# Rotary embedding on one core: table loads moved to SyncE's queue, four small transfers added on ScalarE's

## The chip, the core and the metric

The kernel runs on one core of a Trainium2 chip. The metric is the device time of one execution in microseconds (us), lower is better. The span of a profile, from its first to its last instruction, is a little shorter than that time. Five engines take part: TensorE (PE in the profile), VectorE (DVE), ScalarE (ACT), GpSimd (POOL) and SyncE (SP). Sixteen DMA engines move data between HBM and the on-chip memory. A transfer is issued by one of the instruction engines into its own queue: SyncE's is q1 in the profile, ScalarE's is q10.

## What is computed

```python
# x: (16, 512, 1024) float32, cos and sin: (512, 32) float32, 16 heads of 64
x = x.reshape(batch, seq, num_heads, head_dim)
x1, x2 = x[..., :half_dim], x[..., half_dim:]
cos, sin = cos[None, :, None, :], sin[None, :, None, :]
rotated = np.concatenate([x1 * cos - x2 * sin, x1 * sin + x2 * cos], axis=-1)
```

Every head's vector of 64 is split into two halves of 32, which are rotated by an angle that depends on the position alone. 33.5 MB are read and 33.5 MB are written; the two tables have 64 KB each.

## The kernel before

x is cut into eight tiles of 4 MB. A tile has 128 partitions (2 batches of 64 row groups), and each partition holds 8 rows (k) of 1024 numbers. Five tile buffers exist, so the first five tiles are loaded at once, and the last three wait for the stores of the first three tiles. The result is written over the tile and stored from there.

```python
NB = 2
BUFS = 5
PE_ROWS = ((0, 4), (0, 4))   # rows whose sum is made by TensorE
DVE_B = ((0,), (0,))         # row whose sin product is made by VectorE
FIRST = (3, 8)               # the first tile is loaded in two parts: 3 rows, then 5
LAST_OUT = (4, 8)            # the last tile is stored in two halves
# [...] views, pools
    load(0, 0, FIRST[0])                                      # L73: nc.sync.dma_start
    sin_sb = bp.tile([P, dim], FP32, name="b")[:PB, : KK * half]
    cos_sb = bp.tile([P, dim], FP32, name="b")[:PB, : KK * half]
    nc.scalar.dma_start(out=sin_sb, in_=sin_v)                # L82
    nc.scalar.dma_start(out=cos_sb, in_=cos_v)                # L83
    for lo, hi in zip(FIRST, FIRST[1:]):
        load(0, lo, hi)
    for t in range(1, BUFS):
        load(t)
```

The tables are spread over the 128 partitions by TensorE, with a matrix that repeats each of 64 rows twice; VectorE then makes a signed copy of the sin table. Everything after that needs these tables.

```python
    nc.tensor.matmul(out=sin_t, lhsT=spread, rhs=sin_sb, start=True, stop=True)    # L104
    nc.tensor.matmul(out=cos_t, lhsT=spread, rhs=cos_sb, start=True, stop=True)    # L105
    nc.vector.tensor_scalar_mul(out=sns[:, :, 0, :], in0=sin_k, scalar1=-1.0)      # L107
    nc.vector.tensor_copy(out=sns[:, :, 1, :], in_=sin_k)                          # L108
```

In the main loop GpSimd multiplies a row, with its halves swapped, by the signed sin table (L165). VectorE multiplies by cos (L183) and adds the two (L145). For rows 0 and 4 of each tile the sum is made by TensorE in PSUM (L178) and copied back by ScalarE (L179); for row 0 VectorE makes the sin product as well (L176).

```python
    for t in range(NT):                     # NT = 8 tiles
        xt = tiles[t]
        for k in range(KK):                 # KK = 8 rows
            # [...] the row's work, as above
            if k == 0 and t > 0:
                finish(t - 1)               # store of tile t-1; after tile 2's, the loads of tiles 5 to 7
            add(1)
    finish(NT - 1)

    def store(t, lo=0, hi=KK):
        s = slice(lo * dim, hi * dim)
        nc.sync.dma_start(out=out_v[t][:, s], in_=tiles[t][:, s])                  # L77
```

All loads of x and all stores are issued by SyncE, in program order.

Of the kernel before, what the change touches and what calls it, by code (L numbers as in the profile page):

```python
# [8 lines left out]
FP32 = mybir.dt.float32  # L9
# [12 lines left out]

FIRST = (3, 8)
LAST_OUT = (4, 8)


@with_exitstack
def kernel(
# [13 lines left out]
    nc = tc.nc  # L42
# [7 lines left out]
    NT = batch // NB  # L50
# [4 lines left out]
    cos_v = cos.rearrange("(p k) j -> p (k j)", k=KK)  # L55
    sin_v = sin.rearrange("(p k) j -> p (k j)", k=KK)

    fixed = ctx.enter_context(tc.tile_pool(name="fixed", bufs=1))
# [10 lines left out]
    def load(t, lo=0, hi=KK):  # L69
        if tiles[t] is None:  # L70
            tiles[t] = xp.tile([P, F], FP32, name="xt")
        s = slice(lo * dim, hi * dim)
        nc.sync.dma_start(out=tiles[t][:, s], in_=x_v[t][:, s])  # L73
# [5 lines that stand above are left out]
    load(0, 0, FIRST[0])  # L79
    sin_sb = bp.tile([P, dim], FP32, name="b")[:PB, : KK * half]  # L80
    cos_sb = bp.tile([P, dim], FP32, name="b")[:PB, : KK * half]
    nc.scalar.dma_start(out=sin_sb, in_=sin_v)  # L82
    nc.scalar.dma_start(out=cos_sb, in_=cos_v)  # L83
    for lo, hi in zip(FIRST, FIRST[1:]):
        load(0, lo, hi)
    for t in range(1, BUFS):
# [6 lines left out]
    for i in range(3):  # L93
        ps = pe.tile([P, BANK], FP32, name="ps")
        nc.tensor.matmul(out=ps, lhsT=zero[:, :P], rhs=zero, start=True, stop=True)  # L95

    sns = fixed.tile([P, KK, 2, half], FP32)
    tab = pfix.tile([P, BANK], FP32)
    cos_t = tab[:, : KK * half]
# [14 lines left out]
    def cos_b(k, n):  # L114
        c = cos_t[:, k * half : (k + 1) * half]
        return bass.AP(tensor=c.tensor, offset=c.offset, ap=[c.ap[0], [0, n], [1, half]])

    def over_heads(s):
        return bass.AP(tensor=s.tensor, offset=s.offset, ap=[s.ap[0], [0, nh], [1, hd]])

    def swapped(r, n):
        return bass.AP(
            tensor=r.tensor, offset=r.offset + half, ap=[r.ap[0], [hd, n], [-half, 2], [1, half]]
        )

    def swapped_signed(k):

        i = on_dve.index(k)
        s = sns_t[:, i * hd : (i + 1) * hd]
        return bass.AP(  # L130
            tensor=s.tensor, offset=s.offset + half, ap=[s.ap[0], [0, nh], [-half, 2], [1, half]]
        )

    def pairs(r):
        return r.rearrange("p (a j) -> p a j", j=half)

    def halves(r):
        return r.rearrange("p (h a j) -> p h a j", a=2, j=half)
# [3 lines left out]
    def add(most):  # L142
        while len(pending) > most:
            r, ps, b = pending.pop(0)
            nc.vector.tensor_tensor(out=r, in0=ps, in1=b, op=ALU.add)  # L145

    def finish(t):
        add(0)
        lo = 0
        for hi in LAST_OUT if t == NT - 1 else (KK,):  # L150
            store(t, lo, hi)
            lo = hi
        if t + 1 == NT - BUFS:
            for n in range(BUFS, NT):
                load(n)

    for t in range(NT):
        xt = tiles[t]
        for k in range(KK):
            r = xt[:, k * dim : (k + 1) * dim]  # L160
            own = k in DVE_B[t % 2]
            if not own:
                b = bp.tile([P, dim], FP32, name="b")
                sk = sns[:, k].rearrange("p a j -> p (a j)")
                nc.gpsimd.tensor_tensor(out=halves(b), in0=swapped(r, nh), in1=over_heads(sk), op=ALU.mult)  # L165
            if k in PE_ROWS[t % 2]:
                parts = []
                for c in range(0, dim, BANK):
                    ps = pe.tile([P, BANK], FP32, name="ps")
                    rc = r[:, c : c + BANK]  # L170
                    nc.vector.tensor_tensor(  # L171
                        out=pairs(ps), in0=pairs(rc), in1=cos_b(k, BANK // half), op=ALU.mult
                    )
                    parts.append((ps, rc, swapped(rc, BANK // hd) if own else b[:, c : c + BANK]))
                if own:
                    nc.vector.tensor_tensor(out=halves(r), in0=halves(r), in1=swapped_signed(k), op=ALU.mult)  # L176
                for ps, rc, rhs in parts:
                    nc.tensor.matmul(out=ps, lhsT=ident, rhs=rhs, start=False, stop=True, skip_group_check=True)  # L178
                    nc.scalar.copy(out=rc, in_=ps)  # L179
            else:  # L180
                add(1)
                ps = pd.tile([P, dim], FP32, name="pd")
                nc.vector.tensor_tensor(out=pairs(ps), in0=pairs(r), in1=cos_b(k, 2 * nh), op=ALU.mult)  # L183
                pending.append((r, ps, b))
            if k == 0 and t > 0:
                finish(t - 1)
            add(1)
    finish(NT - 1)


# [33 lines left out]
```

## Time and profile before

| what | value | from |
|---|---|---|
| time, median of 3 | 165.22 us (165.15 to 165.28) | the times |
| span of the profiled execution | 163.5 us | page, first line |
| VectorE busy | 141.4 us (86%) | page, part 1 |
| GpSimd busy | 130.3 us (80%) | page, part 1 |
| TensorE busy | 62.6 us (38%) | page, part 1 |
| ScalarE busy | 20.0 us (12%) | page, part 1 |
| moved | 67.26 MB, mean 411 GB/s | page, part 2 |
| sin table, issue to landing | 7.3 us | page, part 6 |
| cos table, issue to landing | 10.9 us | page, part 6 |
| last two stores of 2 MB, issue to landing | 7.2 us (median) | page, part 6 |

Busy times of different engines lie beside each other and don't add up. A group of instructions is shown with its line in the kernel, its engine, what it writes and reads, its count, its busy time, and in brackets the idle time of the engine ahead of it with what ended that idle time. "DMA" in such a bracket is the landing of a transfer. The chain that ended last is followed back from the last instruction; here it holds VectorE's lines 183, 145, 171 and 176, and the wait at the close of the program (L219). For a window of the span, the profile gives each engine's busy time, the granted TensorE clock, the mean busy share of the 16 DMA engines and what they moved; a packet counts in the window in which it starts.

### The profile page before, as it was taken

The numbers are of one execution on the slowest core, as the hardware profiler recorded it, in microseconds if no ns is written. First come the engines' busy times: TensorE is split into PE (matmuls) and PEld (weight loads), VectorE is DVE, ScalarE is ACT, GpSimd is POOL, SyncE is SP. The second block draws the span as 40 slices with busy tenths as digits, with TensorE's granted clock in tenths as the row PEclk, the third lists the DMA queues.
The fourth block names the chain that finished last, engine by engine and source line by source line (L and its number), as shares of the span: only waits on it lengthen the run. The fifth ranks groups of instructions, "written<-read, shape, count | busy, mean of one in ns | idle before, by whom it ended". The sixth has DMA issues, their size and how long they took to land. (4 is left out here: it accounts for less than half of the span.)

```text
span 163.5 us, 523 instructions
## 1 busy us (share of the span) xinstructions
PE 62.6 (38%) x71; PEld 19.9 (12%) x71; DVE 141.4 (86%) x142; ACT 20.0 (12%) x33; POOL 130.3 (80%) x62
## 2 busy tenths in 40 slices
PE   3022736071804453172608090546217350809000
PEld 0011211020202020111102020202011200202000
DVE  1006999999999999999999999999999999999900
ACT  0210112011110202020201110021102020112000
POOL 1004999999999999999999999998999979970000
PEclk9999999659555555555555559576856786585555
DMA  5999999999989999999999999999999999999994
GB/s 186 443 393 420 489 409 393 497 393 425 473 385 457 441 387 481 409 401 497 361 393 401 489 393 459 425 385 393 393 465 425 425 457 401 393 401 393 433 397 196
DMA packets 2754, 67.26 MB, mean 411 GB/s; under 512 B 320, under 2 KB 448, under 8 KB 448
## 3 DMA queue, kind: packets, MB, share of 16 engines
q1 hardware_dynamic: 2592, 67.11, 97.0%
q10 hardware_dynamic: 160, 0.13, 0.2%
q14 instruction: 2, 0.02, 0.0%
HBM read 33.69 MB, written 33.55 MB: 411 GB/s over the span
## 5 line engine op out<-in xcount | busy, mean ns | idle before, releaser
L165 POOL TENSOR_TENSOR b<-xt,sns 128x1024 f32<-128x1024 f32 x56 | 129.6, 2355 | 15.5 <-DVE sns L108 13.1
L183 DVE TENSOR_TENSOR pd<-xt,tab 128x1024 f32<-128x1024 f32 x48 | 58.1, 1225 | 0.8
L145 DVE TENSOR_TENSOR xt<-pd,b 128x1024 f32<-128x1024 f32 x48 | 58.3, 1217 | 0.0
L178 PE MATMUL ps<-xt,ident 128*128 128x512 f32 x32 | 29.5, 1078 | 48.9 <-issue 45.0
L178 PE MATMUL ps<-b,ident 128*128 128x512 f32 x32 | 29.2, 1067 | 29.7 <-DVE ps L171 27.2
L179 ACT COPY xt<-ps 128x512 f32<-128x512 f32 x32 | 18.7, 586 | 124.1 <-PE ps L178 124.1
L171 DVE TENSOR_TENSOR ps<-xt,tab 128x512 f32<-128x512 f32 x32 | 20.5, 687 | 0.0
L178 PEld LDWEIGHTS ps<-xt,ident 128*128 128x128 f32 x32 | 9.4, 324 | 68.0 <-issue 63.4
L178 PEld LDWEIGHTS ps<-b,ident 128*128 128x128 f32 x32 | 9.2, 317 | 49.9 <-POOL b L165 25.6
L107 DVE TENSOR_SCALAR sns<-tab 128x256 f32<-128x256 f32 x1 | 0.4, 424 | 11.9 <-PE tab L105 11.9
L176 DVE TENSOR_TENSOR xt<-xt,tab 128x1024 f32<-128x1024 f32 x8 | 9.8, 1221 | 0.4
L104 PE MATMUL tab<-b,spread 64*128 64x256 f32 x2 | 1.2, 698 | 5.5 <-DMA b<-in_sin_dram 5.5
L105 PE MATMUL tab<-b,spread 64*128 64x256 f32 x2 | 1.2, 712 | 2.9 <-DMA b<-in_cos_dram 2.9
L179 ACT ACT_TABLE_LOAD x1 | 1.3, 1283 | 7.3 <-DMA xt<-in_x_dram 7.3
L95 PE MATMUL ps<-zero 128*128 128x512 bf16 x3 | 1.5, 626 | 1.2 <-DVE zero L92 1.2
L104 PEld LDWEIGHTS tab<-b,spread 64*128 64x128 f32 x2 | 0.5, 308 | 6.4 <-issue 6.4
L92 DVE MEMSET zero<- 128x256 uint32 x1 | 0.3, 272 | 0.9 <-PEq L205 0.9
L105 PEld LDWEIGHTS tab<-b,spread 64*128 64x128 f32 x2 | 0.5, 307 | 3.7 <-DMA b<-in_cos_dram 3.7
L103 DVE COPY spread<-ident 64x64 f32<-64x64 f32 x2 | 0.3, 183 | 0.2 <-POOL ident masks.py:199 0.2
L95 PEld LDWEIGHTS <-zero 128*128 128x128 bf16 x3 | 0.3, 123 | 1.5 <-DVE zero L92 1.2
masks.py:197 POOL MEMSET ident<- 128x128 f32 x1 | 0.2, 204 | 0.3 <-POOLq L205 0.3
L108 DVE COPY sns<-tab 128x256 f32<-128x256 f32 x1 | 0.4, 415 | 0.0
(6 smaller groups left out, 0.9 us busy)
## 6 DMA issues: line engine op xcount, KB each, us to landing
xt<-in_x_dram SPq DMA_DIRECT2D x7, 4096.0 KB, 31.1
out_dram<-xt SPq DMA_DIRECT2D x7, 4096.0 KB, 20.1
out_dram<-xt SPq DMA_DIRECT2D x2, 2048.0 KB, 7.2
xt<-in_x_dram SPq DMA_DIRECT2D x1, 2560.0 KB, 12.6
xt<-in_x_dram SPq DMA_DIRECT2D x1, 1536.0 KB, 6.5
b<-in_sin_dram ACTq DMA_DIRECT2D x1, 64.0 KB, 7.3
b<-in_cos_dram ACTq DMA_DIRECT2D x1, 64.0 KB, 10.9
```

The source lines that it names most:

```text
L95: nc.tensor.matmul(out=ps, lhsT=zero[:, :P], rhs=zero, start=True, stop=True)
L104: nc.tensor.matmul(out=sin_t, lhsT=spread, rhs=sin_sb, start=True, stop=True)
L105: nc.tensor.matmul(out=cos_t, lhsT=spread, rhs=cos_sb, start=True, stop=True)
L107: nc.vector.tensor_scalar_mul(out=sns[:, :, 0, :], in0=sin_k, scalar1=-1.0)
L108: nc.vector.tensor_copy(out=sns[:, :, 1, :], in_=sin_k)
L145: nc.vector.tensor_tensor(out=r, in0=ps, in1=b, op=ALU.add)
L165: nc.gpsimd.tensor_tensor(out=halves(b), in0=swapped(r, nh), in1=over_heads(sk), op=ALU.mult)
L171: nc.vector.tensor_tensor(out=pairs(ps), in0=pairs(rc), in1=cos_b(k, BANK // half), op=ALU.mult)
L176: nc.vector.tensor_tensor(out=halves(r), in0=halves(r), in1=swapped_signed(k), op=ALU.mult)
L178: nc.tensor.matmul(out=ps, lhsT=ident, rhs=rhs, start=False, stop=True, skip_group_check=True)
L179: nc.scalar.copy(out=rc, in_=ps)
L183: nc.vector.tensor_tensor(out=pairs(ps), in0=pairs(r), in1=cos_b(k, 2 * nh), op=ALU.mult)
```

## The change

The two table loads move from ScalarE's queue to SyncE's, at the same place in the program: behind the first part of the first tile and ahead of its second part. The aim is that the tables come in order, right after the first rows, and not in turns with the second part. After the fourth tile's rows, four small transfers are added on ScalarE's queue: they bring 15, 14, 12 and 8 rows of 16 numbers (64 bytes each) of the sin table into a spare buffer that nothing reads. The program then has 24 transfers where it had 20.

```diff
+SMALL = (15, 14, 12, 8)
...
     load(0, 0, FIRST[0])
     sin_sb = bp.tile([P, dim], FP32, name="b")[:PB, : KK * half]
     cos_sb = bp.tile([P, dim], FP32, name="b")[:PB, : KK * half]
-    nc.scalar.dma_start(out=sin_sb, in_=sin_v)
-    nc.scalar.dma_start(out=cos_sb, in_=cos_v)
+    nc.sync.dma_start(out=sin_sb, in_=sin_v)
+    nc.sync.dma_start(out=cos_sb, in_=cos_v)
     for lo, hi in zip(FIRST, FIRST[1:]):
         load(0, lo, hi)
...
+    spare = fixed.tile([16, len(SMALL), 16], FP32)
     sns = fixed.tile([P, KK, 2, half], FP32)
...
             if k == 0 and t > 0:
                 finish(t - 1)
             add(1)
+        if t == NT // 2 - 1:
+            for i, n in enumerate(SMALL):
+                nc.scalar.dma_start(out=spare[:n, i], in_=sin_v[:n, :16])
     finish(NT - 1)
```

## The prediction

> **What bounds the kernel now.** I read the page's slices and queues first, then the opening of the timeline, then SyncE's waits, then the end in small windows. The page shows the transfers close to full all the way:
>
> ```profile
> DMA  5999999999989999999999999999999999999994
> ...
> q1 hardware_dynamic: 2592, 67.11, 97.0%
> q10 hardware_dynamic: 160, 0.13, 0.2%
> ```
>
> The row of nines is the share of the 16 DMA engines at work. q1 is SyncE's queue (all of x and out), q10 ScalarE's (the two tables). VectorE is at 86%, so there are two candidates for the bound, and the second is visible in the opening:
>
> ```profile
> 8.15 1.19 PE L104 MATMUL tab<-b,spread 64*128 64x256 f32 x2 [5.50 <-DMA b<-in_sin_dram]
> 12.29 0.50 PEld L105 LDWEIGHTS tab<-b,spread 64*128 64x128 f32 x2 [3.67 <-DMA b<-in_cos_dram]
> 12.29 1.22 PE L105 MATMUL tab<-b,spread 64*128 64x256 f32 x2 [2.95 <-DMA b<-in_cos_dram]
> 13.54 0.42 DVE L107 TENSOR_SCALAR sns<-tab 128x256 f32<-128x256 f32 x1 [11.92 <-PE tab L105]
> ```
>
> VectorE starts at 13.54 us because cos lands at 12.2 us (issued at 1.29, 10.9 us to landing). From there it hardly pauses: 9.9 us busy in every 10 us window until the last add ends at about 155.7. What SyncE waits for:
>
> ```profile
> SPq L77 <- DVE xt L145: 132.3, 9, 26.7
> SPq L73 <- DMA out_dram<-xt: 10.9, 2, 9.3
> SPq L219 <- DMA out_dram<-xt: 6.3, 1, 6.3
> ```
>
> All nine stores are issued as VectorE finishes a tile, and the span ends with the landing of the last one. So far it looks like a VectorE chain with 6.6 us of store behind it. The windows at the end correct that:
>
> ```profile
> 130.00:140.00 10.00, 3.34 (x5) 1.16 (x4) 9.84 (x10) 1.17 (x2) 8.89 (x5) 0.67 0.99 429
> 140.00:145.00 5.00, 3.05 (x4) 0.69 (x3) 4.97 (x5) 1.17 (x2) 4.78 (x3) 0.73 0.78 334
> ...
> 155.00:157.00 2.00, 0.00 (x0) 0.00 (x0) 0.72 (x1) 0.00 (x0) 0.00 (x0) 0.50 0.73 311
> ```
>
> The last two columns are DMA share and GB/s. The engines as a group lose 0.22 x 5 = 1.1 us at 140 to 145 and 0.27 x 2 = 0.5 us at 155 to 157, 1.6 us in all; elsewhere their share is about 1. The next view is of 138 to 146 us, in slices of 0.2 us:
>
> ```profile
> GB/s 655 655 492 164 0 492 819 655 492 164 0 164 0 0 328 0 0 2130 164 0 328 0 0 2130 164 0 328 0 0 1802 492 0 328 0 0 1311 983 0 328 0
> ```
>
> A packet of 32 KB counts in the slice in which it starts: 164 is one packet, 328 two, 2130 thirteen. From 139.0 to 140.0 sixteen packets start, one per engine. From 140.2 to 141.2 only three do: thirteen engines have run out of the sixth store and wait for the seventh, which VectorE releases at 140.64; at 141.4 they start together. Three engines are late and still have old packets. **So thirteen engines wait for VectorE, and three do not wait at all.** How late the slowest is: at 431 GB/s (window 130 to 136) one engine moves 26.9 GB/s, a 32 KB packet takes 1.21 us, and eight of them, one engine's share of 4 MB, 9.7 us. The seventh store takes 12.1 us from issue to landing. With 0.8 us from issue to first packet and about 0.35 us from last packet to landing, 10.9 us are explained; the other 1.2 us are the slowest engine. The last store (2 MB) takes 6.6 us where 0.8 + 4.9 + 0.35 = 6.05 are explained, so 0.55 us of that lateness is left at the end. The end of the span is thus set by one late DMA engine that never idles from 1.8 us on, with VectorE's chain only 0.55 us behind it.
>
> **What the Trainium skill says.** "DMA: Bandwidth & Descriptors", section "Queues, rings and completion order": each DMA engine takes turns between the queues it has work for, packet by packet. The trace agrees: cos has four packets of 1 KB and a count per engine, each between packets of 20 KB, and so takes over 3 us after sin. The same page, "Issuing engines are not separate DMA queues": a transfer runs on the same 16 engines whoever issues it. The table packets will be the same load in q1 that they were in q10. The same page, "Why a DMA increments its semaphore by 16 and not by 1": the number of engines of a transfer is the largest one up to 16 that divides the outer sizes, the lowest-numbered ones. So 15, 14, 12 and 8 rows go to 15, 14, 12 and 8 engines with one packet each: engines 0 to 7 get four small transfers, 8 to 11 three, 12 and 13 two, 14 one, 15 none. No trace here shows such a case yet.
>
> **The change, part by part.** *Tables on SyncE's queue.* They now stand behind the first 1.5 MB of x and ahead of the next 2.5 MB, in order. That first part lands at 7.2 us (0.74 + 6.5) with some table packets between; without those a little earlier. A 1 KB packet with its share of counts took 0.04 us (q10 in the window 0 to 14: 2.8% of 14 x 16 us, over 160 packets), so five of them add 0.2 us: sin at about 7.2, cos at about 7.4 us. Then two groups of matmuls, 1.2 us each, as now: VectorE's L107 at about 7.3 + 1.2 + 1.2 = 9.8 us instead of 13.54. **VectorE starts 3.8 us earlier**, GpSimd with it. The second part of x is needed from row 3 of the first tile on, about 5 us after L107, thus near 15 us, and lands at about 13.8 us as now. Later loads keep their places: the sixth tile's load lands at 93, and VectorE will want it at 9.8 + 1 + 5 x 17.6 = 99. So VectorE should end at about 152, and the last three stores be issued at 137, 146 and 152.
>
> *What that is worth.* The bytes and their order in the queue do not change. Up to 140 us every DMA engine is busy, and stores issued earlier only wait longer behind others. The thirteen engines gain their pauses, 1.0 + 0.45 us, and would be done at about 160.1 instead of 161.5. The slowest has no pause to gain, so it still ends at 162.1 and lands at 162.4. **The 3.8 us of VectorE are worth nothing if that engine stays equally late**, and at most about 2 us if its lateness goes away.
>
> *Four small transfers.* ScalarE reaches them after its second copy of tile 3's row 4, which now ends at 80.9 and will end at about 77. At 0.5 to 0.6 us per issue (0.53 and 0.61 for the tables) it is through by about 80, and its next copy is due near 85, so nothing waits for it. No instruction reads what they bring. Eight packets on an engine at 0.04 us are 0.3 us. It can be more: one 8 KB instruction fetch in the store phase shows what a foreign read costs there:
>
> ```profile
> q14 instruction: 1, 0.01, 1.0%
> ```
>
> In the window 57 to 59 it takes 1.0% of 2 x 16 us, 0.3 us; by the packet records the engine that made it came out 0.7 to 0.8 us late against its neighbours, because the big packet beside it was also stretched (1.69 us for 1.21). At a like surcharge of 0.4 us for each of four reads, engines 0 to 7 could lose up to 2 us. The stores in flight at 77 to 81 us are just such a phase.
>
> *The sum.* 0 from VectorE's earlier start while the late engine rules, with room for -2; +0.1 to +2 from the small transfers if the late engine is one of those they burden, 0 if it is one of the high-numbered ones, which have 1.5 us less to lose. Where engines get late cannot be read off the page: packets are stretched at 79 to 84 us (393 GB/s in 78 to 84) and at 106 to 112 (366 GB/s), just where the queue changes between stores and loads, and those changes stay. I choose a small gain: 165.22 - 0.3 = 164.9 us.
>
> **Rivals.** *VectorE bounds the whole run.* For it: 86% busy, continuous, and the chain of work that ended last is nearly all VectorE. Then 3.8 us come off whole: 161.4 us. Against it: 67.26 MB at 431 GB/s are 156.1 us, which with 1.8 us of start and about 1.4 us of landing and closing is a span of 159.3, only 4.2 us under the present 163.5, and stretched packets use up most of that. *The lateness shrinks.* A different rhythm at the changes of direction could leave no engine 1.2 us behind: 163.2 to 164. *The small reads stall the store stream* on the engines they touch, and nothing hides it, as VectorE's slack does not help a DMA engine: 166 to 167 us. *Tables wait longer than thought* behind the first part of x: then VectorE gains less than 3.8 us, but only after losing all of it would the time move.
>
> **Range and chances.** The middle is the late engine as it is, 164.9. The lower edge, 163.5, takes most of the group's 1.6 us of pauses; the upper edge, 166.7, takes the small reads at nearly full surcharge on a late engine. Faster by over 2% would be under 161.9, which needs almost all stretched packets gone: 0.03. Slower by over 2% would be over 168.5, twice the surcharge that I can argue: 0.05. Within 2%: 0.92.
>
> **What would show it.** L107 near 9.8 us, cos landing before 8 us. The last three stores issued near 137, 146 and 152 and taking longer to land than 12.1 and 7.2 us. The windows 140 to 145 and 155 to 157 with a DMA share near 1. SyncE's last wait clearly above 6.3 us. ScalarE's four issues near 77 to 80. If the time falls by about 3.8 us, the step "the transfers are the bound" was wrong; if it rises by over a microsecond, look for engines of low number that are late after 80 us.

## The result, and the profile after

The changed kernel takes **162.42 us** (162.32 to 162.80, six runs); the ratio to the kernel before is **0.987 (0.983 to 0.990)**. The predicted 164.9 (163.5 to 166.7) was over a microsecond too high even at its lower edge. The span fell from 163.5 to 160.7 us.

The page of the changed kernel, DMA row and queues:

```profile
DMA  5999999999999999999999999999999999999994
...
q1 hardware_dynamic: 2752, 67.24, 97.9%
q10 hardware_dynamic: 98, 0.00, 0.0%
```

The bytes are the same and the row of nines is too; only their end has moved. ScalarE's queue holds 98 packets: 15 + 14 + 12 + 8 = 49 of 64 bytes and 49 counts. The opening of its timeline:

```profile
7.62 1.19 PE L107 MATMUL tab<-b,spread 64*128 64x256 f32 x2 [4.97 <-DMA b<-in_sin_dram]
8.18 0.76 PEld L108 LDWEIGHTS tab<-b,spread 64*128 64x128 f32 x2
8.61 1.06 PE L108 MATMUL tab<-b,spread 64*128 64x256 f32 x2
9.70 0.42 DVE L110 TENSOR_SCALAR sns<-tab 128x256 f32<-128x256 f32 x1 [8.08 <-PE tab L108]
```

The second product now follows the first without waiting for cos, and VectorE's first table step (L107 of before is L110 here) starts at 9.70 us instead of 13.54. SyncE's waits:

```profile
SPq L79 <- DVE xt L148: 125.2, 9, 23.9
SPq L75 <- DMA out_dram<-xt: 14.5, 2, 9.5
SPq L225 <- DMA out_dram<-xt: 7.3, 2, 4.8
```

It waits 7 us less for VectorE and more for the landings of stores: the transfers now come last. The store of tile 2, the third, is issued earlier too, in the kernel before at

```profile
70.04 0.33 SPq L77 DMA_DIRECT2D out_dram<-xt  x1
```

and in the changed kernel at

```profile
66.20 0.33 SPq L79 DMA_DIRECT2D out_dram<-xt  x1
```

The windows at the end, with DMA share and GB/s in the last two columns:

```profile
136.00:140.00 4.00, 3.44 (x4) 0.84 (x3) 4.00 (x4) 1.10 (x2) 3.97 (x2) 0.52 0.95 410
140.00:145.00 5.00, 1.74 (x2) 0.83 (x3) 4.97 (x7) 0.07 (x1) 2.35 (x1) 0.83 0.99 426
...
155.00:157.00 2.00, 0.00 (x0) 0.00 (x0) 0.00 (x0) 0.00 (x0) 0.00 (x0) 0.50 1.09 467
```

The pauses at 140 to 145 and 155 to 157 us are gone. Something else is gone too. These are two windows around changes of direction, that is, places where the queue goes from stores to loads (about 80 us) or from loads to stores (about 108 us), before:

```profile
76.00:88.00 12.00, 5.20 (x6) 2.01 (x7) 11.90 (x13) 1.17 (x2) 12.00 (x6) 0.50 1.04 423
104.00:116.00 12.00, 7.34 (x8) 2.18 (x8) 11.93 (x13) 2.34 (x4) 11.18 (x6) 0.67 0.98 390
```

and after:

```profile
76.00:88.00 12.00, 4.17 (x5) 1.18 (x4) 11.90 (x12) 1.75 (x3) 12.00 (x6) 0.50 0.99 426
104.00:116.00 12.00, 3.87 (x5) 1.18 (x4) 11.90 (x13) 1.75 (x3) 11.84 (x6) 0.50 1.00 431
```

Share divided by GB/s is the engines' time for a byte, whatever falls into the window at its edges. It is 6% longer before than after in the first window (1.04 / 423 against 0.99 / 426) and 8% in the second (0.98 / 390 against 1.00 / 431), which over 12 us each is about 1.6 us by estimate. In the trace's packet records, 32 KB packets took up to 2.5 us in the kernel before and at most 1.7 after, for the usual 1.21. I use one number for it below, **the stretch**: what all large packets took beyond the usual, where that was over 7%, summed from 4.5 us on and divided by 16 engines, an average, as the records don't name the engine. It is 2.04 us per engine before and 0.45 after; 0.2 to 0.4 us of that lies at 6 to 8 us, or in the kernel before at 6 to 12, and is not at issue.

### The profile page after: what moved, and what is told of

Read it like the earlier page. It is cut to its first block, busy times and chain, and to the rows that moved or that the text cites. A ratio compares the mean times of both kernels' runs of the same rounds, so it can differ in the third digit from the quotient of the medians.

```text
span 160.7 us, 531 instructions
## 1 busy us (share of the span) xinstructions
PE 62.1 (39%) x71; PEld 20.0 (12%) x71; DVE 141.4 (88%) x142; ACT 20.0 (12%) x33; POOL 130.3 (81%) x62
## 5 line engine op out<-in xcount | busy, mean ns | idle before, releaser
L110 DVE TENSOR_SCALAR sns<-tab 128x256 f32<-128x256 f32 x1 | 0.4, 425 | 8.1 <-PE tab L108 8.1
L107 PE MATMUL tab<-b,spread 64*128 64x256 f32 x2 | 1.2, 697 | 5.0 <-DMA b<-in_sin_dram 5.0
L107 PEld LDWEIGHTS tab<-b,spread 64*128 64x128 f32 x2 | 0.5, 306 | 5.9 <-issue 5.9
```

## The experiments

The kernel before was run beside each group. Its medians were 164.2 to 165.0 us from group to group, so ratios of different groups agree only to about half a percent. In most groups some of its single runs lie near 164.1 us and most others near 165.0; both its traces are of the second kind, and what the first kind does differently is not known.

### Which part of the change brings the gain

*Tables alone*: both table loads by SyncE, no small transfers.

```diff
-    nc.scalar.dma_start(out=sin_sb, in_=sin_v)
-    nc.scalar.dma_start(out=cos_sb, in_=cos_v)
+    nc.sync.dma_start(out=sin_sb, in_=sin_v)
+    nc.sync.dma_start(out=cos_sb, in_=cos_v)
```

> The kernel before with the two table loads on SyncE's queue and no small transfers. Theory V (VectorE's late start is what held all DMA engines up; the late engine of the first profile was a matter of that execution): the whole gain is here, 1.5 to 2.6 us under before, equal to the changed kernel within 0.2 us, L107 at 9.7 us and DMA share near 1 from 140 us on. Theory R (the small transfers change the rhythm of the queue and keep engines from getting late): at most 0.6 us under before, with packets stretched near 79 to 84 and 106 to 112 us and one engine over 1 us behind the others. Theory M (mixed): about half of the gain.

Measured: 162.53 us, ratio 0.985 (0.983 to 0.986). The whole gain is here.

*Small transfers alone*: tables on ScalarE's queue as before.

```diff
+        if t == NT // 2 - 1:
+            for i, n in enumerate(SMALL):
+                nc.scalar.dma_start(out=spare[:n, i], in_=sin_v[:n, :16])
```

> The kernel before with the four small transfers added and the tables still on ScalarE's queue. Theory V: the same as before within 0.3 us, or slower by the 0.1 to 0.3 us that the packets take. Theory R: faster by 1 us or more, no stretched packets at 79 to 84 us. My prediction's surcharge of 0.4 us per small read would make it 0.5 to 2 us slower.

Measured: 164.99 us, ratio 0.9997 (0.9989 to 1.0005). The small transfers cost nothing that can be measured and bring nothing.

*The two kernels once more*, without edits, for a second trace of each.

> The kernel before, unchanged, for a second trace of it and for the noise of the comparison. Theory V: ratio 1 within 0.3%; the stretched packets at 79 to 84 and 106 to 112 us are gone or elsewhere, as they belong to an execution. Theory R: they are there again at the same places, 393 GB/s or less in 78 to 84 us and 370 or less in 106 to 112.

> The changed kernel, unchanged, on the same chip as the other three. Both theories: 1.5 to 2.6 us under before; its trace again without stretched packets by Theory R, with or without by Theory V.

Measured: before 164.93 us, ratio 0.9997 (0.9988 to 1.0006); after 162.29, ratio 0.983 (0.982 to 0.985). Theory V has the gain right and the stretch wrong. The stretch is 2.13 us in the second trace of before and 2.18 with the small transfers, at the same places, and 0.5 in both kernels with early tables. So it belongs to the kernel and not to the execution, and Theory R's cause, the small transfers, is not it.

### What bounds each kernel

*VectorE held back*: tables alone, with idle copies ahead of L107, and so the start of VectorE and GpSimd set by hand. Four lengths, delay_13 to delay_38, made for 1.3 to 3.8 us (L107 came 1.4 to 4.2 us later than in tables alone); this is the longest.

```diff
+    idle = fixed.tile([P, BANK], FP32)
+    for w in (512, 512, 512, 512, 512, 256):
+        nc.vector.tensor_copy(out=idle[:, :w], in_=tab[:, :w])
     nc.vector.tensor_scalar_mul(out=sns[:, :, 0, :], in0=sin_k, scalar1=-1.0)
```

> Two idle copies, about 1.3 us, ahead of L107. Whichever-is-later: VectorE's last store is issued near 153.2, its packets ready near 154, when the engines come free (153.5 to 154.4): 0 to 0.3 us over tables_only, 1.0% to 1.5% under before. If each us of VectorE counts in full: 1.3 us over tables_only.

> The same with three idle copies, about 2.0 us. If the end is set by whichever is later, the DMA engines' load or VectorE's last add plus 6 us: VectorE ends near 153.9 and the engines come free near 154, so this costs 0 to 0.6 us against tables_only. If each us of VectorE's start counts in full: 1.3 us more, halfway to before. By stretched packets that follow VectorE's rhythm: anything between, with the trace showing how many.

> Four and a half idle copies, about 3.0 us: between delay_20 (free of stretched packets) and delay_38 (2.1 us of them per engine). By the later-of-two rule the time is 1 us over delay_20 and 0.8 under delay_38 whether packets are stretched or not; the trace shows on which side of the change the stretching sets in, and whether it fades in or switches.

> Tables on SyncE's queue, no small transfers, and six idle copies on VectorE ahead of L107, about 3.9 us, so that VectorE and GpSimd start when they do in the kernel before. Theory P (the stretched packets and the lost time both come from when VectorE works and releases stores): as slow as before within 0.3%, packets of over 1.3 us again at 79 to 84 and 106 to 112 us. Theory Q (stretched packets come from tables on a second queue): none of them; DMA engines pause at 141 and 156 us all the same and the end follows VectorE's last add, 0.3 to 0.6 us under before.

*Transfers alone*: the main computation left out, each tile stored as it was loaded. The tables' two products and the signed copy stay in, although the text below says that they are left out.

```diff
     for t in range(NT):
-        # [...] the eight rows of the tile
+        if t > 0:
+            finish(t - 1)
```

> All transfers in the same order, the tables' products and the whole main computation left out, so each tile is stored as loaded: the floor of the transfers. From 67.26 MB at 431 GB/s, 1.8 us of start and 1.4 us of landing and closing: span 159.3, time about 161.0 us. If the transfers alone show stretched packets near 79 and 108 us, these do not come from the engines' work; if none, they do.

Measured, with the start of L107 and the end of the last add from the timelines:

| kernel | L107 at | last add ends | span | stretch | time | ratio to before |
|---|---|---|---|---|---|---|
| transfers alone | - | - | 160.5 | 0.37 | 162.34 | 0.988 (0.986 to 0.990) |
| tables alone | 9.60 | 151.8 | 160.8 | 0.53 | 162.53 | 0.985 (0.983 to 0.986) |
| delay_13 | 11.04 | 153.2 | 161.0 | 0.52 | 162.70 | 0.988 (0.985 to 0.991) |
| delay_20 | 11.90 | 154.1 | 161.5 | 0.35 | 163.32 | 0.994 (0.992 to 0.996) |
| delay_30 | 13.21 | 155.4 | 162.9 | 1.72 | 164.66 | 0.999 (0.997 to 1.001) |
| delay_38 | 13.80 | 156.0 | 163.4 | 2.09 | 165.14 | 1.005 (1.003 to 1.007) |
| before, second trace | 13.5 | 155.7 | 163.2 | 2.13 | 164.93 | 1.000 (0.999 to 1.001) |

Two limits fit all rows. VectorE's: last add plus 7.4 us, taken from delay_20, whose last two adds run from 151.75 us for 2.35 us and whose span is 161.5 us:

```profile
151.75 2.35 DVE L148 TENSOR_TENSOR xt<-pd,b 128x1024 f32<-128x1024 f32 x2
```

This gives 162.8, 163.4 and 163.1 for the last three. The transfers': 160.5 us, measured with the main computation left out. The span is the later of the two, with at most 0.4 us on top where they meet (delay_13: 160.6 against 160.5, measured 161.0). The first 1.4 us of delay cost 0.2 us, the next 0.9 cost 0.6, and after that a microsecond of VectorE costs a microsecond. **The kernel before ends at VectorE's limit, the changed one at that of its transfers**: 160.7 us against 160.5. How far the transfers of the kernel before lie under VectorE's limit depends on the stretch, which comes next.

*Tables ahead of everything*: since nothing should come of a still earlier VectorE.

```diff
-    load(0, 0, FIRST[0])
     # [...]
     nc.sync.dma_start(out=sin_sb, in_=sin_v)
     nc.sync.dma_start(out=cos_sb, in_=cos_v)
+    load(0, 0, FIRST[0])
```

> Tables on SyncE's queue ahead of the first part of x, no small transfers. VectorE can start as soon as that part has landed, near 7.5 us, 3 us earlier still. If the DMA engines are the bound now: the same as tables_only within 0.2 us. If VectorE's start still counts: up to 3 us faster.

Measured: 164.22 us, ratio 1.000 (0.998 to 1.002), which neither expectation held. VectorE's main loop does start earlier (8.55 us) and its last add ends at 149.8, but the transfers lose what they cannot make up. Its windows at the start and at the first change from loads to stores:

```profile
1.80:5.00 3.20, 2.78 (x6) 1.16 (x4) 0.00 (x0) 0.00 (x0) 0.00 (x0) 1.00 0.73 198
48.00:55.00 7.00, 3.19 (x5) 0.97 (x4) 6.97 (x8) 0.92 (x3) 7.00 (x4) 0.74 1.00 376
```

and those of the transfers alone, without ScalarE's column, as that engine does nothing there:

```profile
1.80:5.00 3.20, 0.85 (x2) 0.00 (x0) 0.00 (x0) 0.00 (x0) 1.00 0.96 338
48.00:55.00 7.00, 0.00 (x0) 0.00 (x0) 0.00 (x0) 0.00 (x0) 1.00 1.05 449
```

At the start the missing 140 GB/s over 3.2 us are 0.45 MB, about 1 us at 431 GB/s by estimate: x is issued at 1.96 us instead of 0.73, and the engines' share is 0.73 instead of 0.96. In 48 to 55 us a byte takes 14% more time than with the transfers alone, and the records show 0.9 us of stretch at 50 to 54 us. Why this kernel has it there was not tried; its first store had been issued at 28.9 us, so no store was late.

### Where the stretch comes from

It might follow the engines' reads and writes of the tiles, or the times at which transfers are issued. *Without GpSimd's products*: delay_38 with a constant buffer in their place.

```diff
-                b = bp.tile([P, dim], FP32, name="b")
-                # [...]
-                nc.gpsimd.tensor_tensor(out=halves(b), in0=swapped(r, nh), in1=over_heads(sk), op=ALU.mult)
+                b = same
```

> delay_38 with GpSimd's products left out (VectorE and TensorE add a constant buffer instead, so the sums are of other numbers). If GpSimd's reads of the tile are what stretches packets: none at 79 to 84 and 106 to 112 us. If it is VectorE's or TensorE's traffic, or the times at which stores are issued: stretched as in delay_38, about 2 us per engine in all.

*A clock in place of the work*: main computation left out; VectorE copies inside PSUM and lets each store go by writing one column of its tile.

```diff
+    for t in range(NT - 1):
+        pace(15, 512)
+        nc.vector.tensor_copy(out=tiles[t][:, :1], in_=pa[:, :1])
+        finish(t)
```

> Main computation left out; VectorE only copies inside PSUM as a clock and releases each store near the time at which delay_38 does (34.8, 52.4, 70.0 us and so on). If the times of the stores' issues are what stretches packets: about 2 us per engine in all, at 79 to 84 and 106 to 112 us. If the engines' work on the tiles is: less than 0.6 us per engine in all. In both cases the end follows the last store's issue by about 6 us.

Measured: 1.92 us of stretch without GpSimd (one run, 166.04 us). The clock ran slow, 19.7 us a tile instead of 17.6, so its time (one run, 180.86 us) and its end say nothing; but with no work on the tiles beyond that column it has 2.17 us of stretch, at the same two changes, which come 5 us later here. Its windows there:

```profile
81.00:93.00 12.00, 0.00 (x0) 0.00 (x0) 11.65 (x11) 0.00 (x0) 1.00 0.99 393
110.00:122.00 12.00, 0.00 (x0) 0.00 (x0) 11.72 (x11) 0.00 (x0) 1.00 0.98 393
```

In time per byte that is some 8% more than after the change, so it is the issues. In every trace with the stretch at these places, the store of tile 2 was issued less than 3 us before the second store landed by the trace's landing records, when its packets were all but used up: 2.4 us before (kernel before; 2.3 in its second trace and with the small transfers), 2.2 (delay_38), 2.7 (delay_30), 1.3 (no GpSimd), after it (the clock). In every trace without it, 4.0 us (delay_20) or more; 6.2 after the change. Two kernels part this from lateness as such.

*Late work, filled queue*: delay_38 with tile 2 stored in two halves, the first at 61.6 us.

```diff
             add(1)
+            if t == 2 and k == 5:
+                store(2, 0, 4)
     # [...] finish(2) then stores rows 4 to 7 alone
```

> delay_38 with tile 2 stored in two halves, the first as soon as its four rows are done, near 63 us, so that at 70 us there are still about 5 us of packets queued ahead of the second half. All work stays late. Theory Dry: stretched packets gone, 0.6 us per engine or less, no engine late at 140 us. The time stays near delay_38 within 0.4 us, as VectorE's last add plus 7.4 us still sets the end. Theory Work: 2 us of stretched packets per engine as in delay_38.

Measured: 165.03 us, ratio 1.004 (1.002 to 1.005), stretch 0.44. The stretch is gone, with VectorE as late as ever. The time has hardly moved from delay_38's, as the later limit is VectorE's: last add at 155.7, plus 7.4, is 163.1; span 163.0. The loads of tiles 5 to 7 are issued as late as in the kernel before, so it is not they that bring the stretch:

```profile
61.62 8.72 SPq L77 DMA_DIRECT2D out_dram<-xt  x2
70.45 12.19 SPq L73 DMA_DIRECT2D xt<-in_x_dram  x3
```

Tile 2's store has packets of 16 KB here instead of 32, which this kernel alone does not tell apart from the earlier issue. Its windows, with the time per byte of the changed kernel again:

```profile
76.00:88.00 12.00, 5.25 (x6) 2.01 (x7) 11.90 (x13) 1.17 (x2) 12.00 (x6) 0.50 1.02 438
104.00:116.00 12.00, 7.51 (x8) 2.35 (x8) 11.93 (x13) 2.25 (x4) 11.20 (x6) 0.50 0.99 426
```

*Early work, one late store*: tables alone, the store of tile 2 and the loads behind it moved back. The first try moved the store in the program.

```diff
-            if k == 0 and t > 0:
+            if k == (2 if t == 3 else 0) and t > 0:
                 finish(t - 1)
```

> tables_only with one thing changed: the store of tile 2, and with it the loads of tiles 5 to 7, is issued two rows later, near 70.5 us instead of 66.1, under 1 us before the second store's packets end (71.1). All work stays early. Theory Dry (a store that is issued when less than about two packets per engine are left ahead of it makes packets stretch at the next changes of direction): about 1.6 us of stretched packets per engine come back at 79 to 84 and 106 to 112 us, and as the DMA engines are the bound here, the time rises by 1 to 1.7 us over tables_only. Theory Work (it is the phase of the engines' work or of the other issues): no more than 0.6 us of stretched packets per engine, time as tables_only within 0.3 us.

Measured: 162.62 us, ratio 0.990 (0.987 to 0.993), stretch 0.44. It says nothing for or against: the store went out at 67.4 us, as it waits for its data and not for its place in the program. The second try makes the data late, and only these.

```diff
-            if k == 0 and t > 0:
+            if k == 0 and t > 0 and t != 3:
                 finish(t - 1)
+            if k == 3 and t == 3:
+                nc.vector.tensor_copy(out=tiles[2][:, :1], in_=tiles[2][:, :1])
+                finish(2, keep=1)
     # [...] with keep, finish leaves tile 3's pending adds alone
```

> late_st2 moved its store only to 67.4 us, as the store waits for data and not for its place in the program. Here VectorE copies one column of tile 2 onto itself during row 3 of tile 3, and the store of tile 2 and the loads behind it wait for that: issued near 70.7 us, some 0.4 us before the second store's packets end. All other work and issues stay early. Theory Dry: 1.2 to 1.8 us of stretched packets per engine at 79 to 84 and 106 to 112 us, time 1 to 1.7 us over tables_only, 0.2% to 0.7% under before. Theory Work: 0.6 us of stretched packets or less, time as tables_only within 0.4 us.

Measured: **164.85 us, ratio 1.000 (0.999 to 1.001)**, stretch 2.19. SyncE's issues in 60 to 90 us, and the same windows:

```profile
71.09 0.33 SPq L77 DMA_DIRECT2D out_dram<-xt  x1
71.54 12.06 SPq L73 DMA_DIRECT2D xt<-in_x_dram  x3
84.04 0.34 SPq L77 DMA_DIRECT2D out_dram<-xt  x1
```

```profile
76.00:88.00 12.00, 4.41 (x5) 1.18 (x4) 11.90 (x12) 1.76 (x3) 12.00 (x6) 0.72 0.99 393
104.00:116.00 12.00, 4.01 (x5) 1.17 (x4) 11.90 (x12) 1.75 (x3) 12.00 (x6) 0.64 1.00 401
```

One store held for 5 us takes the whole gain away, though VectorE starts at 9.77 and ends at 152.0 as in the fast kernel. About half a microsecond of that is an empty queue at 71 us (0.53 us per engine by the records), the other 1.7 us are stretch. VectorE's limit would be 152.0 + 7.4 = 159.4; that of the transfers, 160.5 + 0.5 + 1.7 = 162.7, is near the span of 163.0.

So most of the gain needs two things at once. Late work without stretch (half_st2) takes 165.03 us, early work with stretch (late_st2_held) 164.85, of which 0.5 is the empty queue; late work with stretch (delay_38) takes 165.14. Only early work without stretch (tables alone) takes 162.53.

Why packets stretch at the next two changes of direction, up to 40 us after the queue was short, stays open; that they do, and that an earlier store of tile 2 prevents it here, is shown.

No version beat the changed kernel by more than the comparison can tell.

## Why the prediction was wrong, point by point

- **VectorE's start: right.** L107 near 9.8 us predicted, 9.70 measured; last stores at 137, 146 and 152 predicted, 136.8, 146.0 and 152.0 measured.
- **The queue stays full to the end and becomes the limit: right.** The DMA share stays near 1 where it had paused, and the transfers alone take the same time.
- **"The slowest has no pause to gain, so it still ends at 162.1": wrong, and this is the step that failed.** It rested on "those changes stay". The changes of direction stayed; the stretched packets at them did not. The slowest engine's last count (the packet that reports its share as moved) ended at 159.4 us, the others' from 158.3 us on instead of the 160.1 that I gave them. I had taken lateness for a property of the order of transfers, which I knew to be unchanged. It follows from when they are issued, and the earlier start moved that too: the third store from 70.0 to 66.2 us. With VectorE early and that one issue moved to 71.1 us, a microsecond later than in the kernel before, the time is 164.85 us, close to the predicted 164.9; half a microsecond of it is the empty queue.
- **"The end of the span is thus set by one late DMA engine": true of one execution, not of the kernel.** In the first trace the engines' last packets end from 161.55 to 161.70 us and one at 162.09. In the second trace no engine is late: all end from 161.58 to 161.71, and the time is about the same (164.96 us). VectorE's limit, 155.7 + 7.4 = 163.1, already explains the second trace's span of 163.2; the late engine added 0.35 us in the first. I saw two limits 0.55 us apart and let the later one decide alone, as if moving the one could not move the other.
- **The small transfers: mis-sized.** I gave 0.1 to 2 us; measured 0.0 (ratio 0.9997 with them, 0.9997 without). In the window 80 to 89 us, where their packets run, q10 takes 0.7% of 9 x 16 us over 98 packets, 0.01 us each and not 0.04. The surcharge of the 8 KB instruction fetch did not carry over to reads of 64 bytes. ScalarE issued them at 76.5 to 79.4 us, as predicted, and no copy was late. The rule of the Trainium skill for how many engines a transfer uses ("DMA: Bandwidth & Descriptors", "Why a DMA increments its semaphore by 16 and not by 1") agrees with the trace as to the number of engines: the four landings count up in 15, 14, 12 and 8 late steps, one for each engine that carried a packet. Which engines these were, the trace doesn't say.
- **The rivals.** "The lateness shrinks" was the right direction, with 163.2 to 164 too little: I let one engine catch up with the others, but the 16 engines lost 1.6 us of stretch each on average, and their pauses as well. "VectorE bounds the whole run" was right for the kernel before and would have given 161.4; the transfers' floor stopped it 1 us short. My own estimate of that floor, a span of 159.3, was 1.2 us under the 160.5 measured.

## What to carry to other kernels

Where two limits lie within a microsecond or two, work out each by itself, and measure the lower one with a kernel that leaves the other out: here the transfers alone gave the end of the changed kernel to 0.2 us. Before a slow stretch in a trace is taken as fixed, ask what else the change moves in it, above all when transfers are issued. Keep work queued ahead of the DMA engines; here a lead of 4 us was enough and one of under 3 us was not. If a store comes too late for that, the part of the tile that is done can be stored first: that took the stretch away in half_st2, though no time, as VectorE was last there.

## What the runs showed of the hardware that I had not expected

A store issued when the packets ahead of it were almost used up (under 3 us to the landing of the store before) was followed by longer packets at the next change from stores to loads, and again at the one from loads to stores nearly 30 us later: 14 to 32 packets of 32 KB at each, up to 2.5 us for the usual 1.21 (2.7 in delay_30), 1.3 to 1.8 us per engine in all. With 4.0 us and more there was next to none at these places. It came with no engine at work on the data but for one column a tile (pace_late). A short queue is not the only thing that brings it: with the tables at the head of the queue, 0.9 us came at 50 to 54 us with no store late. These tables of 2 x 64 KB also cost the transfers about 1 us at the start by estimate; behind the first 1.5 MB of x the same window has 338 GB/s instead of 198.
